# Mixing layers of a two-block network: the order of VectorE's rotation, the recurrence's products and two weight splits

## The chip, the cores and the metric

The kernel runs on one core of one Trainium2 chip. The metric is the device time of one execution in microseconds (us), lower is better. The core has a matrix engine (TensorE, PE in the profile), a vector engine (VectorE, DVE), a scalar engine (ScalarE, ACT), GpSimd (POOL), and SyncE (SP), which issues the DMAs.

## The reference, cut to what matters

A first block (attention, pooling, a mixture of 32 experts) is followed by a second block of two layers. Only the mixing part of each of these two layers is touched by the change:

```python
def second_block(x, positions, attn_norm_w, w_in, ..., w_out, ...):
    for layer in range(2):
        h = rms_norm_2(x, attn_norm_w[layer])                    # x: (1, 256, 1024)
        a_q, a_i, a_zf, a_zb, a_g, b_u, c_q, c_k, c_v = jnp.split(h @ w_in[layer], SPLIT_POINTS, axis=-1)
        o_a = hgrn2_mixer(a_q, a_i, a_zf, a_zb, a_g, lb_all[layer])   # a gated recurrence, both directions
        o_b = fourier_mixer(b_u)
        o_c = dilated_attention_mixer(c_q, c_k, c_v, positions)       # q, k rotated; 8 heads of 64
        x = x + jnp.concatenate([o_a, o_b, o_c], axis=-1) @ w_out[layer]
        ...                                                           # squared-ReLU feed-forward
    return rms_norm_2(x, final_norm_w)
```

## The kernel before, in words

All products are made in fp32r, with each operand as a high part and a low part. `split` makes them for a 128x1024 piece of the weights: ACT writes the high part `wh`, DVE the low part `wl` (L203, two instructions of 128x512 where a norm weight is folded in; L207, one of 128x1024, for `w_out`). Four pairs of `wh`/`wl` buffers take turns.

`mix_layer` runs six projections one after the other: `proj(512)` z, `proj(0)` q and i of the recurrence, `proj(1536)` Q, `proj(2048)` K, `proj(2560)` V, `proj(1024)` gate and Fourier input, and then the output projection by `w_out`. A projection has four blocks on PE, each of 12 matmuls of 128x512 (L230 to L232: `wh` twice, `wl` once, for two row tiles and two slices), with one `split` each. Here the blocks behind the K projection are called **A, B, C, D** (V) and **E, F, G, H** (gate); the names of their low parts are `wl_5307`, `5403`, `5450`, `5534`, `5586`, `5655`, `5693`, `5744`.

After each block, `bg()` advances every generator in the list `bgs` by one step and so puts other work between the blocks:

- `hgrn`, the recurrence as eight levels `lv` 0 to 7. A level is `qt` (DVE, L1509) and `kt` (POOL, L1513), then small matmuls (`hsm`, L1483, up to level 4; `diag`, L1526, levels 5 and 6; `cross`, level 7), for `hsm` a masked copy `sl` (DVE, L1490) and its sum `sd` (POOL, L1491), and the updates `hES` (L1545) and `hIP` (L1546) on DVE for the next level.
- `turn`, of Q and of K. The evacuation `evac_rot` multiplies the projection by cosine and sine on DVE (`rx` L1605, `rt` L1606, two row tiles) and adds the two (L1607: the first tile on POOL, the second on DVE). `turn` transposes the result on PE (`prot`, L1617) and copies it on ACT.
- `attention`, in four softmax pieces called here **a, b, c, d** (tiles `s_5386`, `5432`, `5517`, `5563`; sums `l_5392`, `5438`, `5523`, `5569`): scores on PE (`sc` L1643), scale and mask on DVE (L1648), maximum on DVE (L1651), its negative on POOL (L1652), exp on ACT (L1656), reciprocal on DVE (L1657), and four multiplications on POOL (L1660). Then, for each of two groups, `values`: transposes of the weights on PE (`pt` L1671), copies `pT` on DVE and ACT (L1672), and the product with V (`po` L1680).

Every engine takes its instructions in a fixed order, which a scheduler settles when the kernel is built, from the order of the code, priorities and dependences; an instruction that waits holds up all behind it on its engine. The layer 1 part repeats that of layer 0, 310.3 us later.

Of the kernel before, what the change touches and what calls it, by code (L numbers as in the profile page):

```python
# [115 lines left out]
class Kernel:  # L116
    def __init__(self, tc, a):
# [2 lines left out]
        self.last_load = None  # L120
        self.smalls = []


    def add_ring(self, st, n, cols=4096, **kw):

# [89 lines left out]
    def halves(self, v, g=None):  # L215

        for hh in range(2):
            hi, lo = self.split(v[:, 2 * hh:2 * hh + 2, :].rearrange("p k f -> p (k f)"),
                                g if g is None else g[:, 2 * hh:2 * hh + 2])
            for k2 in range(2):  # L220
                yield 2 * hh + k2, hi, lo, k2 * 512

# [1176 lines left out]
    def mix_layer(self, layer, rc, late):  # L1399
# [3 lines left out]
        with ExitStack() as st:  # L1403
# [6 lines left out]
            hT, mT = self.hT, self.mT  # L1410
            win = a["w_in_2"][layer]
            gw = self.norm_cols("attn_norm_w_2", 1) if layer else self.g0
            tk = {}

            def tok(name, n=512, tag="tk", bufs=2):
                tk[name] = p.tile([128, 2, n], F32, name=name, tag=tag, bufs=bufs)
# [32 lines left out]
            def hgrn():  # L1449
# [50 lines left out]
                for lv in range(8):  # L1500
# [5 lines left out]
                        return x.rearrange("p n (b w h) -> p (n b) w h", w=2, h=h)[:, :, w]  # L1506

                    for d in range(2):
                        nc.vector.tensor_tensor(half(qt, 1 - d), half(qd, 1 - d), half(IP[:, d], 1 - d), op=ALU.mult)  # L1509
                        if lv == 0:  # L1510
                            nc.scalar.copy(half(kt, d), half(kk[:, d], d))
                        else:
                            nc.gpsimd.tensor_tensor(half(kt, d), half(kk[:, d], d), half(ES[:, d], d), op=ALU.mult)  # L1513
# [25 lines left out]
                    if lv < 7:  # L1539

                        for d in range(2):
                            edge = (lambda x: x[:, :, h - 1:h]) if d == 0 else (lambda x: x[:, :, 0:1])
                            full = [128, 2 * S // (2 * h), h]
                            ip, es = IP[:, d], ES[:, d]
                            nc.vector.tensor_tensor(half(es, d), half(es, d), edge(half(ip, 1 - d)).to_broadcast(full), op=ALU.mult)  # L1545
                            nc.vector.tensor_tensor(half(ip, 1 - d), half(ip, 1 - d), edge(half(ip, d)).to_broadcast(full), op=ALU.mult)  # L1546
                    yield
                while not tail:
# [49 lines left out]
            def evac_rot(dst, gens, steps):  # L1598

                def g(c0, ps):  # L1600
                    rx = p.tile([128, 2, 8, 2, 32], F32, name="rx", tag="rx", bufs=1)
                    for t in range(2):
                        x = ps[t].rearrange("p (h w c) -> p h w c", h=8, w=2)
                        tmp = p.tile([128, 8, 2, 32], F32, name="rt", tag="rt", bufs=2)
                        nc.vector.tensor_tensor(rx[:, t], x, cos[:, t].unsqueeze(1).unsqueeze(1).to_broadcast([128, 8, 2, 32]), op=ALU.mult)  # L1605
                        nc.vector.tensor_tensor(tmp, swapped(x), sin[:, t].unsqueeze(1).to_broadcast([128, 8, 2, 32]), op=ALU.mult)  # L1606
                        (nc.vector if t else nc.gpsimd).tensor_tensor(rx[:, t], rx[:, t], tmp, op=ALU.add)  # L1607

                    def turn():
                        for _ in range(steps):  # L1610
                            yield
                        for m in range(0, 4, 2):
                            ps = bank((128, 2, S), "prot")
                            for i in range(2):
                                for t in range(2):
                                    src = rx[:, t, 2 * (m + i):2 * (m + i) + 2].rearrange("p h w c -> p (h w c)")
                                    nc.tensor.transpose(ps[:, i, t * 128:(t + 1) * 128], src, self.ident)  # L1617
                            nc.scalar.copy(dst[:, m:m + 2], ps)
                        yield
                    gens.insert(0, turn())  # L1620
                return g

            def evac_cv(c0, ps):
# [37 lines left out]
                    yield  # L1661

            def values(g):
                pTs = []
                for kt in range(2):
                    pT = p.tile([128, 2, 2, S], F32, name="pT", tag="pT", bufs=2)
                    for j in range(2):
                        pt = bank((128, 2, S), "pt")
                        for t in range(2):
                            for i in range(2):  # L1670
                                nc.tensor.transpose(pt[:, i, t * 128:(t + 1) * 128], probs[g][t][:, j, i, kt * 128:(kt + 1) * 128], self.ident)  # L1671
                        (nc.scalar.copy if j else nc.vector.tensor_copy)(pT[:, j], pt)  # L1672
                    pTs.append(pT)
                    yield
                po = bank((128, 2, S), "po2")
                for i in range(2):
                    for kt in range(2):
# [32 lines left out]
                    into_mT(2 + m, ps)  # L1710
                yield

            bgs, tail = [], []

            def bg():
                for w in list(bgs):
                    if next(w, 0) == 0:
                        bgs.remove(w)

            def proj(c0, e, late=()):  # L1720
                ps = [bank() for _ in range(2)]
                self.tok_part(ps, hT, win, 0, c0, True, False, bg, g=gw[:, 0:4])
                for f in late:
                    f()
                self.tok_part(ps, hT, win, 4, c0, False, True, bg, g=gw[:, 4:8])
                e(c0, ps)

            proj(512, evac_z, late)
            if not layer:
# [5 lines left out]
            hg = hgrn()  # L1735
            bgs.append(hg)
            proj(0, evac_qi)
            proj(1536, evac_rot(qT, bgs, 1))
            proj(2048, evac_rot(kT, bgs, 0))
            att = attention()  # L1740
            bgs.append(att)
            proj(2560, evac_cv)
# [5 lines left out]
            bg()  # L1748
            wo = a["w_out_2"][layer]
            acc = [[bank(name="wo") for _ in range(2)] for _ in range(2)]  # L1750
            for n in range(2):
                self.tok_part(acc[n], mT, wo, 4, n * 512, True, False, bg)
            while bgs:
# [148 lines left out]
```

## Time and profile before

| | us |
|---|---|
| median of 3 runs (1305.76 to 1309.66) | 1307.24 |
| the profiled execution | 1306.97 |
| its span (first to last instruction) | 1305.2 |
| PE busy in the span | 1253.0 |
| DVE busy | 680.5 |
| ACT busy | 510.7 |
| POOL busy | 200.7 |

The mean granted TensorE clock of the span is 0.989 of full speed. PE is busy 96% of the span, so what can be won or lost is idle time of PE, time at a lower clock, and the order in which other engines release it. A timeline row has the start of a group of like instructions, the time from its first start to its last end, engine, line, and in brackets the idle time before it with what ended it. Neighbouring instructions overlap a little, so that the distance between two starts is less than the first one's duration.

### The profile page before, as it was taken

The page shows a single profiled execution, that of the slowest core. Times are in us where ns is not written, and L with a number is a line of the kernel's source. Part 1 is how long each engine was busy: PE and PEld are TensorE (multiplying, and loading weights), DVE is VectorE, ACT ScalarE, POOL GpSimd, SP SyncE. Part 2 cuts the span into 40 slices and gives each one's busy share as a digit, 9 for nine tenths or more (in the row PEclk, how much of TensorE's full clock was granted, in tenths as well). Part 3 has the DMA queues.
Part 4 walks back from the last instruction along what each step waited for, and adds up shares of the span by engine and source line. Part 5 has one row for each costly group of instructions (what it writes and reads, how often), then busy time and mean ns, then how long its engine had stood idle before and what let it go on. Part 6 is the DMA issues. An engine that isn't in the chain of part 4 may idle for free. (4 is left out here: it accounts for less than half of the span.)

```text
span 1305.2 us, 19758 instructions
## 1 busy us (share of the span) xinstructions
PE 1253.0 (96%) x7985; PEld 875.2 (67%) x7985; DVE 680.5 (52%) x1164; ACT 510.7 (39%) x919; POOL 200.7 (15%) x270
## 2 busy tenths in 40 slices
PE   6999988999999999899999999999999999999997
PEld 3889976344443443333357678998988767989896
DVE  3698797122122221212157965655557994765654
ACT  2456433111110111101056465555556555655544
POOL 0011030000000000000024541211113461211211
PEclk9999998999999999999999999999999999999999
DMA  9998797999999999999975342655554423555550
GB/s 326 372 340 276 266 381 266 409 416 429 426 429 427 426 427 427 426 428 421 419 305 187 114 130 90 223 181 186 193 193 158 161 82 126 188 177 193 193 162 33
DMA packets 102597, 359.37 MB, mean 275 GB/s; under 512 B 8772, under 2 KB 17856, under 8 KB 87656
## 3 DMA queue, kind: packets, MB, share of 16 engines
q1 hardware_dynamic: 101832, 357.00, 72.1%
q8 instruction: 63, 1.03, 0.3%
q0 software_dynamic: 480, 1.07, 0.2%
q14 instruction: 30, 0.25, 0.1%
q10 hardware_dynamic: 192, 0.02, 0.0%
HBM read 357.00 MB, written 1.06 MB: 274 GB/s over the span
## 5 line engine op out<-in xcount | busy, mean ns | idle before, releaser
L207 DVE TENSOR_TENSOR wl<-w,wh 128x1024 fp32r<-128x1024 f32 x128 | 156.5, 1227 | 100.9 <-ACT wh L206 100.9
L206 ACT CAST wh<-w 128x1024 fp32r<-128x1024 f32 x128 | 134.1, 1050 | 144.4 <-PE up L241 65.8
L202 ACT ACTIVATE wh<-w,vcols 128x512 fp32r<-128x512 f32 x176 | 121.2, 718 | 78.9 <-PE dn L231 34.7
L203 DVE SCALAR_TENSOR_TENSOR wl<-w,vcols,wh 128x512 fp32r<-128x512 f32 x176 | 131.1, 778 | 36.5 <-ACT wh L202 34.4
L241 PE MATMUL up<-hT,wh 128*128 128x256 f32 x512 | 142.4, 278 | 0.0
L242 PE MATMUL up<-hT,wl 128*128 128x256 f32 x512 | 142.4, 279 | 0.0
L240 PE MATMUL up<-hT,wh 128*128 128x256 f32 x512 | 142.4, 278 | 0.0
L1015 PE MATMUL pu<-w,xT 128*64 128x512 f32 x512 | 121.5, 608 | 5.4 <-DMA w<-in_w_expert_up_dram 5.4
L1015 PE MATMUL pg<-w,xT 128*64 128x512 f32 x512 | 119.5, 604 | 0.0
L1101 ACT CAST yh<-y 128x512 fp32r<-128x512 f32 x32 | 19.8, 618 | 253.6 <-DVE y L1100 187.9
L1015 PE MATMUL py<-w,actT 128*64 128x512 f32 x480 | 108.0, 593 | 1.4 <-DMA w<-in_w_expert_down_dram 1.4
L231 PE MATMUL dn<-wh,actl 128*128 128x512 f32 x256 | 101.3, 396 | 0.0
L230 PE MATMUL dn<-wh,acth 128*128 128x512 f32 x256 | 101.2, 395 | 0.0
L232 PE MATMUL dn<-wl,acth 128*128 128x512 f32 x256 | 101.2, 396 | 0.0
L241 PEld LDWEIGHTS up<-hT,wh 128*128 128x128 f32 x512 | 96.9, 189 | 0.6
L240 PEld LDWEIGHTS up<-hT,wh 128*128 128x128 f32 x512 | 96.2, 188 | 0.6
L242 PEld LDWEIGHTS up<-hT,wl 128*128 128x128 f32 x512 | 96.0, 188 | 0.5 <-DVE wl L203 0.5
L1803 POOL TENSOR_TENSOR relu<-relu 128x256 f32<-128x256 f32 x64 | 53.6, 838 | 265.9 <-ACT relu L1802 265.9
L230 PE MATMUL b<-wh,hT 128*128 128x512 f32 x224 | 92.0, 412 | 2.4 <-ACT wh L202 1.9
L232 PE MATMUL b<-wl,hT 128*128 128x512 f32 x224 | 89.4, 403 | 2.3 <-DVE wl L207 1.5
L1100 DVE SCALAR_TENSOR_TENSOR y<-py,ws,gate 128x512 f32<-128x512 f32 x30 | 22.5, 751 | 128.7 <-PE py L1015 127.2
L1015 PEld LDWEIGHTS pu<-w,xT 128*64 128x64 f32 x512 | 38.0, 139 | 76.9 <-issue 67.1
(411 smaller groups left out, 2273.3 us busy)
## 6 DMA issues: line engine op xcount, KB each, us to landing
w<-in_w_expert_up_dram SPq DMA_DIRECT2D x26, 2048.0 KB, 25.7
w<-in_w_expert_down_dram SPq DMA_DIRECT2D x26, 2048.0 KB, 27.2
w<-in_w_expert_gate_dram SPq DMA_DIRECT2D x24, 2048.0 KB, 25.4
w<-in_w_in_dram SPq DMA_DIRECT2D x40, 1024.0 KB, 6.5
w<-in_w_up_dram SPq DMA_DIRECT2D x32, 1024.0 KB, 5.4
w<-in_w_down_dram SPq DMA_DIRECT2D x32, 1024.0 KB, 5.0
w<-in_w_ada_dram SPq DMA_DIRECT2D x24, 1024.0 KB, 9.8
w<-in_w_expert_gate_dram SPq DMA_DIRECT2D x16, 1024.0 KB, 10.3
```

The source lines that it names most:

```text
L202: self.nc.scalar.activation(hi[:, c], v[:, c], AF.Copy, scale=g[:, i:i + 1])
L203: self.nc.vector.scalar_tensor_tensor(lo[:, c], v[:, c], g[:, i:i + 1], hi[:, c].bitcast(F32), op0=ALU.mult, op1=ALU.subtract)
L206: self.last_hi = self.nc.scalar.copy(hi, v).ins
L207: self.last_lo = self.nc.vector.tensor_tensor(lo, v, hi, op=ALU.subtract).ins
L230: nc.tensor.matmul(ps, hT.tok(0, k, t), wh, start=first, stop=False)
L231: nc.tensor.matmul(ps, hT.tok(1, k, t), wh, start=False, stop=False)
L232: nc.tensor.matmul(ps, hT.tok(0, k, t), wl, start=False, stop=last)
L240: nc.tensor.matmul(o, hi[:, c], hT.mov(0, k), start=first and m % 2 == 0, stop=False, skip_group_check=True)
L241: nc.tensor.matmul(o, hi[:, c], hT.mov(1, k), start=False, stop=False, skip_group_check=True)
L242: nc.tensor.matmul(o, lo[:, c], hT.mov(0, k), start=False, stop=last and m % 2 == 1, skip_group_check=True)
L1015: queue["last"] = f(*args, **kw).ins
L1803: nc.gpsimd.tensor_tensor(r, r, r, op=ALU.mult)
```

## The change

It has three parts, alike in both layers. (1) In the projections of Q and K, `turn` stands behind the recurrence in `bgs` and takes one step more before it transposes, and the last `bg()` of the projection runs behind the evacuation (`first=True`). (2) `behind(...)` holds an instruction behind given ones in the issue order of its engine: the recurrence's `qt` and `hES` behind the latest rotation's last add (`turned[-1:]`, on DVE), and the second split of the next projection behind the same add (`split_after[1]`). (3) The first split of the output projection is held behind the `pT` copies of the first group's second half (`split_after[0]`).

```diff
+    def behind(self, *ins):
+        st = ExitStack()
+        for i in ins:
+            st.enter_context(self.tc.issue_after(i))
+        return st
...
         for hh in range(2):
-            hi, lo = self.split(v[:, 2 * hh:2 * hh + 2, :].rearrange("p k f -> p (k f)"),
-                                g if g is None else g[:, 2 * hh:2 * hh + 2])
+            with self.behind(*self.split_after.pop(hh, ())):
+                hi, lo = self.split(v[:, 2 * hh:2 * hh + 2, :].rearrange("p k f -> p (k f)"),
+                                    g if g is None else g[:, 2 * hh:2 * hh + 2])
...
-            tk = {}
+            tk, turned = {}, []
...
-                        nc.vector.tensor_tensor(half(qt, 1 - d), half(qd, 1 - d), half(IP[:, d], 1 - d), op=ALU.mult)
+                        with self.behind(*turned[-1:]):
+                            nc.vector.tensor_tensor(half(qt, 1 - d), half(qd, 1 - d), half(IP[:, d], 1 - d), op=ALU.mult)
...
-                            nc.vector.tensor_tensor(half(es, d), half(es, d), edge(half(ip, 1 - d)).to_broadcast(full), op=ALU.mult)
+                            with self.behind(*turned[-1:]):
+                                nc.vector.tensor_tensor(half(es, d), half(es, d), edge(half(ip, 1 - d)).to_broadcast(full), op=ALU.mult)
...
-                        (nc.vector if t else nc.gpsimd).tensor_tensor(rx[:, t], rx[:, t], tmp, op=ALU.add)
+                        last = (nc.vector if t else nc.gpsimd).tensor_tensor(rx[:, t], rx[:, t], tmp, op=ALU.add).ins
+                    turned.append(last)
+                    self.split_after[1] = (last,)
...
-                    gens.insert(0, turn())
+                    gens.insert(1, turn())
...
-                        (nc.scalar.copy if j else nc.vector.tensor_copy)(pT[:, j], pt)
+                        copies.append((nc.scalar.copy if j else nc.vector.tensor_copy)(pT[:, j], pt).ins)
                     pTs.append(pT)
                     yield
+                if not g:
+                    copied.extend(copies[2:])
...
-            def proj(c0, e, late=()):
+            def proj(c0, e, late=(), first=False):
...
-                self.tok_part(ps, hT, win, 4, c0, False, True, bg, g=gw[:, 4:8])
+                steps = [bg]
+                if not first:
+                    steps.append(bg)
+                self.tok_part(ps, hT, win, 4, c0, False, True, lambda: steps and steps.pop()(), g=gw[:, 4:8])
                 e(c0, ps)
+                if first:
+                    bg()
...
-            proj(1536, evac_rot(qT, bgs, 1))
-            proj(2048, evac_rot(kT, bgs, 0))
+            proj(1536, evac_rot(qT, bgs, 2), first=True)
+            proj(2048, evac_rot(kT, bgs, 1), first=True)
...
+            self.split_after[0] = copied
```

The order on PE differs only around the two rotations. At that of K, behind block A of layer 0 (`b_5303` and `b_5304` are the two row tiles of the V projection, `rx` the rotated K), before:

```order
L1617 MATMUL prot_5324<-ident_69,rx_5294 128x128
L1617 MATMUL prot_5330<-ident_69,rx_5294 128x128
L1483 MATMUL hsm_5336<-qt_5288,kt_5289 32x32 x8
L1617 MATMUL prot_5324<-ident_69,rx_5294 128x128 x3
L1617 MATMUL prot_5330<-ident_69,rx_5294 128x128 x3
L1483 MATMUL hsm_5336<-qt_5288,kt_5289 32x32 x8
L1483 MATMUL hsm_5356<-qt_5288,kt_5289 32x32 x16
L1643 MATMUL sc_5380<-kT_4680,qT_4679 128x256
L1643 MATMUL sc_5381<-kT_4680,qT_4679 128x256
L1643 MATMUL sc_5380<-kT_4680,qT_4679 128x256
L1643 MATMUL sc_5381<-kT_4680,qT_4679 128x256
L230 MATMUL b_5303<-wh_5402,hT00_78 128x512
```

and of the change, from the second of the four `wh` matmuls of block B (its first `wl` matmul is the last row):

```order
L240 MATMUL b_5303<-wh_5402,hT10_80 128x512
L239 MATMUL b_5304<-wh_5402,hT00_78 128x512
L240 MATMUL b_5304<-wh_5402,hT10_80 128x512
L1492 MATMUL hsm_5324<-qt_5297,kt_5298 32x32 x16
L1492 MATMUL hsm_5344<-qt_5297,kt_5298 32x32 x16
L1630 MATMUL prot_5368<-ident_69,rx_5288 128x128 x4
L1630 MATMUL prot_5374<-ident_69,rx_5288 128x128 x4
L1656 MATMUL sc_5380<-kT_4680,qT_4679 128x256
L1656 MATMUL sc_5381<-kT_4680,qT_4679 128x256
L1656 MATMUL sc_5380<-kT_4680,qT_4679 128x256
L1656 MATMUL sc_5381<-kT_4680,qT_4679 128x256
L241 MATMUL b_5303<-wl_5403,hT00_78 128x512
```

The first four matmuls of block B have moved ahead of the recurrence and the transposes, and the recurrence ahead of the transposes. At the rotation of Q it is the same without `sc`, where before the transposes stood behind a whole block and the recurrence another block later.

On DVE the rotation now stands ahead of `qt` and `hES`, and this moves what follows. Around the third reciprocal (`l_5523`, piece c), before:

```order
L1657 RECIPROCAL l_5523<-l_5523 128x4
L1545 TENSOR_TENSOR hES_4677<-hES_4677,hIP_4676 128x4x64
L1651 TENSOR_REDUCE mx_5566<-s_5563 128x4
L1546 TENSOR_TENSOR hIP_4676<-hIP_4676 128x4x64
L1545 TENSOR_TENSOR hES_4677<-hES_4677,hIP_4676 128x4x64
L203 SCALAR_TENSOR_TENSOR wl_5744<-w_4683,g0_748,wh_5743 128x512
L1546 TENSOR_TENSOR hIP_4676<-hIP_4676 128x4x64
L203 SCALAR_TENSOR_TENSOR wl_5744<-w_4683,g0_748,wh_5743 128x512
L1672 COPY pT_5641<-pt_5642 128x512
L1509 TENSOR_TENSOR qt_5761<-hq_4678,hIP_4676 128x2x128
```

and of the change:

```order
L1670 RECIPROCAL l_5523<-l_5523 128x4
L1556 TENSOR_TENSOR hES_4677<-hES_4677,hIP_4676 128x8x32
L1664 TENSOR_REDUCE mx_5566<-s_5563 128x4
L1557 TENSOR_TENSOR hIP_4676<-hIP_4676 128x8x32
L1556 TENSOR_TENSOR hES_4677<-hES_4677,hIP_4676 128x8x32
L211 SCALAR_TENSOR_TENSOR wl_5655<-w_4683,g0_748,wh_5654 128x512
L1557 TENSOR_TENSOR hIP_4676<-hIP_4676 128x8x32
L1685 COPY pT_5641<-pt_5642 128x512
L1670 RECIPROCAL l_5569<-l_5569 128x4
L211 SCALAR_TENSOR_TENSOR wl_5655<-w_4683,g0_748,wh_5654 128x512
```

Where the split of block H (`wl_5744`) stood between the third reciprocal and the fourth, the split of block F (`wl_5655`) stands now, its first half between them and its second half behind the fourth (`l_5569`); before, F's split stood ahead of the second reciprocal. The recurrence's updates there are those of one level earlier.

On POOL, from the multiplications of piece a on, before:

```order
L1660 TENSOR_SCALAR s_5386<-s_5386,l_5392 128x256 x4
L1491 TENSOR_TENSOR sd_4965<-sd_4965,sl_5484 128x128
L1491 TENSOR_TENSOR sd_4965<-sd_4965,sl_5504 128x128
L1513 TENSOR_TENSOR kt_5673<-hk_4675,hES_4677 128x4x64 x2
L1660 TENSOR_SCALAR s_5432<-s_5432,l_5438 128x256 x4
L1652 TENSOR_SCALAR mx_5520<-mx_5520 128x4
L1660 TENSOR_SCALAR s_5517<-s_5517,l_5523 128x256 x4
L1652 TENSOR_SCALAR mx_5566<-mx_5566 128x4
L1513 TENSOR_TENSOR kt_5762<-hk_4675,hES_4677 128x2x128 x2
L1660 TENSOR_SCALAR s_5563<-s_5563,l_5569 128x256 x4
```

and of the change:

```order
L1673 TENSOR_SCALAR s_5386<-s_5386,l_5392 128x256 x4
L1500 TENSOR_TENSOR sd_4965<-sd_4965,sl_5484 128x128
L1500 TENSOR_TENSOR sd_4965<-sd_4965,sl_5504 128x128
L1673 TENSOR_SCALAR s_5432<-s_5432,l_5438 128x256 x4
L1523 TENSOR_TENSOR kt_5552<-hk_4675,hES_4677 128x8x32 x2
L1665 TENSOR_SCALAR mx_5520<-mx_5520 128x4
L1673 TENSOR_SCALAR s_5517<-s_5517,l_5523 128x256 x4
L1665 TENSOR_SCALAR mx_5566<-mx_5566 128x4
L1673 TENSOR_SCALAR s_5563<-s_5563,l_5569 128x256 x4
L1523 TENSOR_TENSOR kt_5673<-hk_4675,hES_4677 128x4x64 x2
L1523 TENSOR_TENSOR kt_5762<-hk_4675,hES_4677 128x2x128 x2
```

The `kt` of level 5 (8x32) has moved from ahead of piece a to behind piece b, and that of level 6 (4x64) from ahead of piece b to behind piece d. SP's order of loads is as before. The three splits of `w_out` behind the first group's copies now stand together on DVE.

## Rows read from the trace of the kernel before

**Rows 1.** Windows: length, busy PE PEld DVE ACT POOL (count), PEclk, DMA share, GB/s.
```profile
705.00:732.70 27.70, 27.70 (x368) 21.91 (x366) 27.20 (x54) 13.19 (x23) 12.80 (x15) 1.00 0.42 131
...
738.00:740.40 2.40, 2.40 (x56) 1.74 (x56) 2.00 (x5) 0.58 (x1) 1.74 (x4) 0.55 0.02 7
...
765.00:770.00 5.00, 4.00 (x32) 2.50 (x29) 4.56 (x7) 3.13 (x6) 4.78 (x4) 1.00 0.77 236
```

**Rows 2.** Timeline of PE: start, duration, instruction, [idle before <-releaser].
```profile
722.59 1.03 PE L1617 MATMUL prot<-ident,rx 128*128 128x128 f32 x8
...
735.66 0.44 PE L1617 MATMUL prot<-ident,rx 128*128 128x128 f32 x2 [2.90 <-POOL rx L1607]
...
738.62 1.87 PE L1643 MATMUL sc<-kT,qT 64*128 64x256 f32 x8
740.41 0.50 PE L230 MATMUL b<-wh,hT 128*128 128x512 f32 x1
...
743.37 1.13 PE L1643 MATMUL sc<-kT,qT 64*128 64x256 f32 x8
...
747.41 0.76 PE L1483 MATMUL hsm<-qt,kt 64*32 64x32 f32 x64
...
1045.99 0.44 PE L1617 MATMUL prot<-ident,rx 128*128 128x128 f32 x2 [2.90 <-POOL rx L1607]
```

**Rows 3.** Timeline of DVE, same columns.
```profile
732.99 0.68 DVE L1605 TENSOR_TENSOR rx<-b,cosr 128x512 f32<-128x512 f32 x1
...
735.82 0.68 DVE L1607 TENSOR_TENSOR rx<-rx,rt 128x512 f32<-128x512 f32 x1
...
749.28 0.76 DVE L203 SCALAR_TENSOR_TENSOR wl<-w,g,wh 128x512 fp32r<-128x512 f32 x1
...
759.03 0.18 DVE L1657 RECIPROCAL l<-l 128x4 f32<-128x4 f32 x1 [2.44 <-ACT s L1656]
...
761.30 0.88 DVE L203 SCALAR_TENSOR_TENSOR wl<-w,g,wh 128x512 fp32r<-128x512 f32 x1
...
762.44 1.23 DVE L203 SCALAR_TENSOR_TENSOR wl<-w,g,wh 128x512 fp32r<-128x512 f32 x1
...
764.52 0.17 DVE L1657 RECIPROCAL l<-l 128x4 f32<-128x4 f32 x1
```

**Rows 4.** Timeline of POOL, same columns.
```profile
722.59 2.04 POOL L1513 TENSOR_TENSOR kt<-hk,hES 128x256 f32<-128x256 f32 x2
...
734.34 1.26 POOL L1607 TENSOR_TENSOR rx<-rx,rt 128x512 f32<-128x512 f32 x1 [0.69 <-DVE rt L1606]
...
748.01 3.54 POOL L1660 TENSOR_SCALAR s<-s,l 128x256 f32<-128x256 f32 x4
...
752.54 1.42 POOL L1513 TENSOR_TENSOR kt<-hk,hES 128x256 f32<-128x256 f32 x2
753.94 2.71 POOL L1660 TENSOR_SCALAR s<-s,l 128x256 f32<-128x256 f32 x4
...
759.30 2.35 POOL L1660 TENSOR_SCALAR s<-s,l 128x256 f32<-128x256 f32 x4 [2.49 <-DVE l L1657]
...
764.79 4.99 POOL L1660 TENSOR_SCALAR s<-s,l 128x256 f32<-128x256 f32 x4 [0.52 <-DVE l L1657]
```

**Rows 5.** Timeline of PE around the fifth to seventh block.
```profile
753.18 0.51 PE L230 MATMUL b<-wh,hT 128*128 128x512 f32 x1
...
756.15 0.76 PE L1526 MATMUL diag<-qt,kt 64*32 64x32 f32 x64
...
757.69 0.47 PE L230 MATMUL b<-wh,hT 128*128 128x512 f32 x1
...
760.52 1.03 PE L1671 MATMUL pt<-ident,s 128*128 128x128 f32 x8
...
766.79 1.51 PE L1680 MATMUL po<-pT,cv 128*64 128x256 f32 x12 [1.00 <-DVE pT L1672]
```

**Rows 6.** DMA issues, 690 to 800 us: KB each, median us to landing.
```profile
w<-in_w_out_dram SPq DMA_DIRECT2D x4, 1024.0 KB, 5.1
```

More of the change, by code (lines that the diff above doesn't have):

```diff
@@ L121, in __init__ @@
         self.smalls = []
+        self.split_after = {}
+    def behind(self, *ins):
[3 more added lines that the diff above has]
+        return st
     def add_ring(self, st, n, cols=4096, **kw):
@@ L1663, in values @@
             def values(g):
-                pTs = []
+                pTs, copies = [], []
                 for kt in range(2):
@@ L1711, in fourier @@
                 yield
-            bgs, tail = [], []
+            bgs, tail, copied = [], [], []
             def bg():
```

## The prediction

> **What bounds the kernel now.** The engine shares came first: PE is busy for 1253.0 of the span's 1305.2 us (the table above), so a gain can only come from the gaps and the clock. Then the windows of one mixing layer. From 705 to 732.7 us PE has no gap and its granted clock is 1.00 [rows 1]. Then, at the rotation of K, PE idles 2.90 us for the rotation's add [rows 2], and the clock falls to 0.55 from 738 to 740.4 us [rows 1], between the chip's two levels of 1.2 and 2.4 GHz. The same gap stands 310.3 us later in the second layer [rows 2], so everything below counts twice. At the rotation of Q there is none: the transposes at 722.59 us begin at once [rows 2]. The only other gap that the change touches is 1.00 us at the first product with V [rows 5]; no fall of the clock goes with it (1.00 from 765 to 770 us, [rows 1]). Last I followed the softmax through DVE and POOL, because the order rows show it moved: reciprocal c waits 2.44 us for the exp [rows 3], and POOL multiplies in four stretches of 2.35 to 4.99 us [rows 4]. It is a chain with little slack, not counted by PE's share.
>
> Times below are on the axis of layer 0 in the trace of before.
>
> **The change at the two rotations.** Block A starts at 735.66 − 2.90 − 2.83 = 729.93 us (2.83 is one block, 757.69 to 760.52, [rows 5]), and block B ends at 743.37 [rows 2]: 13.4 us. With the change, kt decides when PE goes on: the rotation's first two DVE steps (0.60 each by the starts, row length 0.68, [rows 3]), then POOL's add, 1.26, and two kt, 2.04 [rows 4], make 4.5 us from the start of A, if the rotation starts there. PE arrives after A and the four moved matmuls, 2.83 + 0.92 = 3.75: a wait of 0.75 (0.4 to 1.0, as kt is between 1.42 and 2.04, [rows 4], and the rotation starts a little behind A). Then 0.76 for hsm, 1.03 for eight transposes, 0.4 for the copy of K (none shown here; between 0 and the 0.68 of a 128x512 pass), 1.13 for the scores and 1.83 for the other eight matmuls [rows 2]. The sum is 9.65 us, so K gains 3.8. Q has the same wait, which it did not have, and its splits follow later on DVE: it costs 0.8 (0.5 to 1.5). At the end of B PE is **3.0 us ahead**, and the scores of piece a end at 738.5 instead of 740.41: 1.9 us earlier (1.0 to 4.0, the latter if every wait above vanished). If nothing else moved, the change would gain 3.0 us a layer.
>
> **What lies behind it.** From the end of the first scores to POOL's first multiplication of piece a it takes 748.01 − 740.41 = 7.6 us on DVE, POOL and ACT, and this doesn't get shorter: it starts at about 746.1. Then 4.5 us to the end of a and its two sd (748.01 to 752.54), 2.7 for b and 1.42 for two kt, in before kt first, after it b first, so 754.7 either way for the negated maximum of c [rows 4]. Reciprocal c came 2.4 us after that (756.65 to 759.03), so now at about 757.1. PE meets this line first: block E, 2.97 us, would start at 753.18 − 3.0 and end at 753.2, and the diag behind it now waits for the kt behind b until 754.7. It took 1.54 from diag to F, so F starts at 756.3 [rows 5], only 1.4 us ahead of before. Here half of the lead is gone.
>
> **The new wait.** Block F needs the first half of its low part at its third matmul, 0.46 later, at 756.8. In before that split was made ahead of reciprocal b and waited for nobody. Now it stands behind reciprocal c, two updates of the recurrence and maximum d. In before the split in this place (H's) ended 762.11 − 759.03 = 3.1 us behind reciprocal c [rows 3]; it hid there, since H comes two blocks later. So the half is ready at 757.1 + 3.1 = 760.2, and **PE waits 3.4 us**. The second half stands behind reciprocal d. That came 5.5 us behind c (764.52 − 759.03), and nothing of this changes: maximum d, its negative behind POOL's c, the exps. So d is at 762.6 and the half at 763.4 with one split of 0.76 [rows 3]. PE comes to its use at about 761.9, waits 1.5 more, and ends F with four matmuls at 764.4. In before F ended at 760.52 [rows 5]. F is **3.9 us late**. Its range is 1.8 (scores that end 4.0 instead of 1.9 earlier) to 4.8 (1.0 earlier).
>
> Behind F the low parts of G and H come in one row on DVE, ahead of PE. The diag of level 6 follows a block, a transposition and G later, near 768.1; its kt stands behind POOL's d. That starts 0.27 after reciprocal d and lasts 2.35 to 4.99 us, with 1.42 of kt 766.6 to 769.3 [rows 4]: hidden up to 1.2 us, which I leave to the range. The 1.00 us gap at the product with V goes, because PE is later than the copies: **−1.0**.
>
> The clock: after 2.90 us without work the stretch from 735.66 to 740.41 took 4.75 us, where its rows at full clock (1.03, 0.76, 1.13) make 2.92 [rows 2]. A gap of 1.00 us cost nothing [rows 1]. The new wait of 3.4 us is nearer the former: **+1.6**, with 0 and 3.2 (paid at both waits in F) as bounds; the 1.8 of the old gap also held a short wait. The gain at K above has the end of the old price in it.
>
> The third part of the change, the output projection's splits, puts three passes of 128x1024 together ahead of DVE's copies of the mixed output. PE is busy with other blocks meanwhile: **+0.3** as an estimate, between nothing, where they are hidden, and 1.4, somewhat over the 1.23 of the longest split here (762.44, [rows 3]). The ring of weights is freed later, but a load lands 5.1 us after its issue [rows 6] and SP issues in the same order; its data are used tens of us later. Nothing is charged; if that cover were gone, the price would be F's lag, 3.9 us a layer.
>
> Sum of a layer against before: 3.9 − 1.0 + 1.6 + 0.3 = **4.8 us slower**, two layers 9.6. The profiled execution took 1306.97 us, 0.27 below the median of the runs shown and 1.77 above its span, so 1306.97 + 9.6 = **1316.6 us**.
>
> **A rule that would make it dearer.** The split that PE waits for in F's second half now runs while POOL multiplies d. In the trace a split beside POOL's multiplication took 0.76 us (749.28, with POOL busy from 748.01, [rows 3, 4]), as it does alone, and one beside kt took 1.23 (762.44, [rows 3]). The Trainium skill, "SBUF — State Buffer", section "Who interferes with whom", says that a DVE instruction that reads two SBUF inputs and a GpSimd instruction lock each other out for the whole of whichever came first. The first of the two rows doesn't agree with it for POOL's multiplications, the second does for kt. By the rule the half would wait for one of POOL's four multiplications of d, up to 4.99/4 = 1.2 us, on average 0.6 a layer: 1317.8 us.
>
> **The rivals.**
> - *Faster: the softmax chain runs much quicker once DVE waits.* POOL's multiplications take 0.59 us each in c and 0.88 in a for the same work [rows 4]; if DVE's work beside them is what lengthens them and the kt, and DVE now stands idle before its reciprocals, the chain shrinks. Where it decides: each us by which reciprocals c and d come before 757.1 and 762.6 takes one from F's 3.9, and the 1.6 of the clock falls away; a gain of 2 a layer needs 5.2 us, F wholly on time 6.9. For it: all of a, b and c at c's pace save 1.6 us, and scores that end 4.0 earlier instead of 1.9 save 2.1. Against: that is 3.7, not 5.2, and reciprocal c waits 2.44 us for exps in the trace of before too [rows 3]. With F on time: 3.9 − 6.9 − 1.0 + 0.3 = 3.7 faster a layer, 1299.6 us.
> - *No change: the lead is just eaten.* If POOL's a runs like c (1.2 us less) and its b too (0.4), and the scores come 0.7 earlier than I put them, the reciprocals come 2.3 us earlier; F's first wait is then 1.1, too short for the clock: 4.8 − 2.3 − 1.6 = 0.9 a layer, 1308.8 us.
> - *Dearer: kt of level 6 is late too.* If POOL's d takes its 4.99 us again, the diag waits 1.2 us for kt behind it, and the clock is paid twice (1.6 more) and the tail 1.1 more: 8.5 to 8.7 a layer, 1324 us.
> - *The price is paid by POOL, not DVE.* Were the kt behind b 2.07 instead of 1.42, both diags move by 0.65; it is inside the first forecast's range.
>
> **Numbers.** The forecast, F waits for DVE in both halves, 60%: 1311 to 1320.5 us. Dearer 13%: 1320.5 to 1326. No change in kind, 17%: 1303 to 1311. Faster, 10%: 1296 to 1303. A measurement here can tell 0.3%, 3.9 us, from no change, so 1303.3 to 1311.2 counts as the same. Slower has 73%, the same 17%, faster 10%. The range of eight in ten leaves out the faster case, the lower half of the no-change case and the upper part of the dearer one: 1307.5 to 1322.
>
> **What would show it.** In the trace after: no 2.90 us gap before the transposes of K but a wait under 1.0 before hsm, on POOL's kt, at both rotations; the clock at 1.00 there; the scores of a some 2 us earlier; diag of 32x32 waiting for kt; then two gaps in block F released by DVE's wl of L211, the larger 2 to 4 us, with the clock falling behind it; no gap before the product with V. I am wrong if block F runs without a gap (then reciprocal d is much earlier than 762.6), if PE's gap at the rotations is as long as before, or if the clock doesn't fall behind F's wait (then 3.2 us less).

## The result and the profile after

The changed kernel takes 1321.57 us (median of 4 runs, 1320.04 to 1325.64) against 1307.24: the ratio is 1.011, with a 95% interval of 1.0092 to 1.0128. It is slower, on the forecast's side and inside its range (1307.5 to 1322), but by 14.3 us where 9.6 was forecast.

All of it lies in the two mixing layers, and more than the difference of the two profiles shows. In the trace a layer's **mixing stretch**, from the start of the recurrence's first small products (`hsm<-hq`) to that of the feed-forward's first product (`up`), is 99.48 us before (708.99 to 808.47; second layer 99.46) and 107.62 after (705.88 to 813.50; second layer 107.61): **8.14 us a layer**, 16.3 in both. The feed-forward layers agree to 0.02 us. The first block happened to end some 3 us sooner in the profile after, and such differences of the first block come and go between profiles (the stretch of layer 0 starts at 705.2 to 714.1 us in those of the runs below); the stretch repeats to 0.03 us between the two layers unless the clock falls. So the runs below are read by it, beside their times.

PE's gaps of layer 0 after, those of more than 0.5 us, with the rows that answer to [rows 2] and [rows 5] (the axis is 3.11 us ahead of that of before):

```profile
717.95 0.75 PE L1492 MATMUL hsm<-qt,kt 64*32 64x32 f32 x64 [1.03 <-DVE qt L1519]
...
720.26 0.73 PE L241 MATMUL b<-wl,hT 128*128 128x512 f32 x2 [0.54 <-DVE wl L211]
...
723.53 0.51 PE L241 MATMUL b<-wl,hT 128*128 128x512 f32 x1 [0.70 <-DVE wl L211]
...
734.28 0.75 PE L1492 MATMUL hsm<-qt,kt 64*32 64x32 f32 x64 [0.85 <-DVE qt L1519]
...
747.76 0.50 PE L241 MATMUL b<-wl,hT 128*128 128x512 f32 x1 [1.29 <-DVE wl L211]
...
752.62 0.50 PE L241 MATMUL b<-wl,hT 128*128 128x512 f32 x1 [0.57 <-DVE wl L211]
...
755.12 0.76 PE L1536 MATMUL diag<-qt,kt 64*32 64x32 f32 x64
...
759.88 0.50 PE L241 MATMUL b<-wl,hT 128*128 128x512 f32 x1 [2.51 <-DVE wl L211]
...
762.90 0.80 PE L241 MATMUL b<-wl,hT 128*128 128x512 f32 x1 [0.95 <-DVE wl L211]
...
764.78 1.91 PE L1684 MATMUL pt<-ident,s 128*128 128x128 f32 x8
```

At K the gap of 2.90 us is gone, with 0.85 in its place, and at Q there are now three (1.03, 0.54, 0.70). F waits twice for its split, 2.51 and 0.95. The windows of the same trace tell what the clock did:

```profile
709.50:717.95 8.45, 7.42 (x93) 5.86 (x93) 5.89 (x10) 3.93 (x6) 4.42 (x5) 1.00 0.00 0
734.00:737.30 3.30, 2.78 (x80) 2.21 (x80) 3.30 (x9) 1.07 (x2) 1.79 (x4) 1.00 0.00 0
759.88:764.78 4.90, 3.95 (x11) 2.56 (x12) 3.63 (x8) 2.55 (x9) 2.48 (x4) 0.61 0.16 13
764.78:766.34 1.56, 1.56 (x10) 1.56 (x8) 1.17 (x2) 0.00 (x0) 1.56 (x3) 0.50 1.04 400
```

It stays at 1.00 through the rotations and falls to half behind F's wait: the transposes at 764.78 take 1.91 us instead of 1.03. On DVE, with the rows that answer to [rows 3]:

```profile
710.08 0.58 DVE L1499 TENSOR_TENSOR sl<-hsm,kmix 128x128 f32<-128x128 f32 x2 [3.08 <-PE hsm L1492]
712.61 0.69 DVE L1616 TENSOR_TENSOR rx<-b,cosr 128x512 f32<-128x512 f32 x1 [1.95 <-PE b L241]
...
715.74 2.06 DVE L1519 TENSOR_TENSOR qt<-hq,hIP 128x256 f32<-128x256 f32 x2
...
732.32 1.82 DVE L1519 TENSOR_TENSOR qt<-hq,hIP 128x256 f32<-128x256 f32 x2
...
746.95 1.64 DVE L211 SCALAR_TENSOR_TENSOR wl<-w,g,wh 128x512 fp32r<-128x512 f32 x2
...
756.68 0.18 DVE L1670 RECIPROCAL l<-l 128x4 f32<-128x4 f32 x1 [1.78 <-ACT s L1669]
...
758.95 0.88 DVE L211 SCALAR_TENSOR_TENSOR wl<-w,g,wh 128x512 fp32r<-128x512 f32 x1
...
762.03 0.18 DVE L1670 RECIPROCAL l<-l 128x4 f32<-128x4 f32 x1 [1.27 <-ACT s L1669]
762.12 0.72 DVE L211 SCALAR_TENSOR_TENSOR wl<-w,g,wh 128x512 fp32r<-128x512 f32 x1
...
771.52 3.48 DVE L215 TENSOR_TENSOR wl<-w,wh 128x1024 fp32r<-128x1024 f32 x3
774.92 0.41 DVE L313 TENSOR_TENSOR mT<-po,mT 128x256 fp32r<-128x256 f32 x1
```

DVE now stands idle *ahead* of Q's rotation, 3.08 and 1.95 us: the recurrence's `qt` and `hES`, which it did there before, may not run until the rotation is through. And when they run, a pair of `qt` takes 2.06 and 1.82 us instead of about 0.75. POOL, answering to [rows 4], shows what runs beside it:

```profile
715.23 2.29 POOL L1523 TENSOR_TENSOR kt<-hk,hES 128x256 f32<-128x256 f32 x2
...
731.80 2.04 POOL L1523 TENSOR_TENSOR kt<-hk,hES 128x256 f32<-128x256 f32 x2
...
745.99 2.95 POOL L1673 TENSOR_SCALAR s<-s,l 128x256 f32<-128x256 f32 x4
...
752.00 2.30 POOL L1523 TENSOR_TENSOR kt<-hk,hES 128x256 f32<-128x256 f32 x2
...
762.30 3.52 POOL L1673 TENSOR_SCALAR s<-s,l 128x256 f32<-128x256 f32 x4 [2.42 <-DVE l L1670]
765.80 1.41 POOL L1523 TENSOR_TENSOR kt<-hk,hES 128x256 f32<-128x256 f32 x2
```

The `kt` of 715.23 and 731.80 cover all but the last 0.3 us of those `qt`. From the start of the stretch to the first mixed output (`mT`, 774.92) DVE's gaps in this trace add up to 9.0 us, against 3.2 in the trace of before, and its pass for that output starts 69.04 us into the stretch instead of 59.99, behind three passes of the output projection's split (771.52).

### The profile page after: what moved, and what is told of

Its sections match the earlier page's. It is cut to its first block, busy times and chain, and to the rows that moved or that the text cites. A ratio compares the mean times of both kernels' runs of the same rounds, so it can differ in the third digit from the quotient of the medians.

```text
span 1318.4 us, 19762 instructions
## 1 busy us (share of the span) xinstructions
PE 1255.7 (95%) x7985; PEld 873.7 (66%) x7985; DVE 686.2 (52%) x1164; ACT 510.8 (39%) x919; POOL 199.2 (15%) x270
## 3 DMA queue, kind: packets, MB, share of 16 engines
q8 instruction: 63, 1.03, 0.3%
HBM read 357.00 MB, written 1.06 MB: 272 GB/s over the span
## 5 line engine op out<-in xcount | busy, mean ns | idle before, releaser
L211 DVE SCALAR_TENSOR_TENSOR wl<-w,vcols,wh 128x512 fp32r<-128x512 f32 x176 | 129.1, 767 | 36.7 <-ACT wh L210 34.6
L239 PE MATMUL b<-wh,hT 128*128 128x512 f32 x224 | 92.4, 414 | 2.2 <-ACT wh L210 1.7
L240 PE MATMUL b<-wh,hT 128*128 128x512 f32 x224 | 89.9, 401 | 0.0
```

The lines of the kernel that those rows point to most:

```text
L211: self.nc.vector.scalar_tensor_tensor(lo[:, c], v[:, c], g[:, i:i + 1], hi[:, c].bitcast(F32), op0=ALU.mult, op1=ALU.subtract)
L239: nc.tensor.matmul(ps, hT.tok(0, k, t), wh, start=first, stop=False)
L240: nc.tensor.matmul(ps, hT.tok(1, k, t), wh, start=False, stop=False)
```

## The experiments

The table gives the start of some PE work in layer 0, in us from the start of the stretch, each read as the difference of two starts in a run's trace. A, C, F, G and H are blocks, f is the first Fourier product, up the end of the stretch, in both layers. A stretch is that of one execution, the ratio that of all. For x2 to x7 the two agree to 0.7 us of a kernel; for the change, x1 and x8 to x12 the times are 1.3 to 2.6 us lower against before than the stretches say, and what makes that difference was not looked for.

| run | A | C | F | G | H | f | up, layer 0 / 1 | ratio to before (95%) |
|---|---|---|---|---|---|---|---|---|
| before | 20.86 | 35.44 | 48.70 | 52.32 | 59.25 | 68.56 | 99.48 / 99.46 | |
| the change | 23.72 | 34.60 | 50.78 | 60.46 | 66.83 | 76.70 | 107.62 / 107.61 | 1.011 (1.0092 to 1.0128) |
| x1 order only | 20.86 | 36.50 | 49.74 | 53.37 | 60.41 | 69.71 | 100.64 / 100.26 | 0.9999 (0.9982 to 1.0017) |
| x2 no recurrence hold | 22.10 | 35.78 | 49.02 | 52.64 | 62.20 | 73.02 | 103.96 / 102.40 | 1.0052 (1.0033 to 1.0071) |
| x3 rotation on DVE | 23.21 | 33.54 | 49.96 | 58.03 | 63.75 | 75.90 | 106.86 / 106.72 | 1.011 (1.0091 to 1.0129) |
| x4 K only | 20.88 | 31.74 | 47.95 | 56.18 | 61.88 | 73.89 | 104.83 / 104.81 | 1.0079 (1.006 to 1.0098) |
| x5 F's split first | 23.67 | 34.54 | 50.75 | 54.38 | 62.14 | 74.65 | 105.60 / 106.15 | 1.0093 (1.0073 to 1.0113) |
| x6 K only, F's split first | 20.91 | 31.78 | 47.95 | 51.58 | 59.33 | 71.83 | 102.82 / 102.83 | 1.0053 (1.0032 to 1.0074) |
| x7 holds only | 21.82 | 32.41 | 47.67 | 56.10 | 61.82 | 74.20 | 105.12 / 104.72 | 1.0083 (1.0064 to 1.0102) |
| x8 third part only | 20.87 | 36.64 | 49.92 | 53.55 | 59.62 | 69.37 | 100.31 / 100.01 | 0.9998 (0.9982 to 1.0014) |
| x9 x6, mixed output first | 20.86 | 31.72 | 47.91 | 51.53 | 59.32 | 68.71 | 99.61 / 99.63 | 0.9985 (0.9971 to 0.9999) |
| x10 x9, kt ahead of d | 20.91 | 31.76 | 47.95 | 51.57 | 57.66 | 66.97 | 97.91 / 97.91 | 0.9959 (0.9945 to 0.9974) |
| x11 x10, both rotations | 23.70 | 34.57 | 50.76 | 54.38 | 60.49 | 69.79 | 100.71 / 101.24 | 1.0003 (0.9988 to 1.0018) |
| x12 x10, K's add on DVE | 20.86 | 31.18 | 47.58 | 51.20 | 57.20 | 66.51 | 97.45 / 97.48 | 0.9959 (0.9943 to 0.9976) |

**x1, the order of the generators alone.** The change without `behind(...)` on `qt` and `hES` and without both `split_after`.

> Only the order of the generators is kept (the rotation's transposes behind the recurrence, the last step behind the evacuation); the recurrence's qt and hES, the second split and the output projection's split are held behind nothing. Theory A (the loss comes from what DVE does behind the holds: F's split behind reciprocals c and d, qt beside kt): four matmuls and hsm slide into the old 2.90 us gap at K, F's split is made ahead of reciprocal b as before, no gap in block F; 1.5 to 3.5 us a layer faster than before, 1300 to 1304 us. Rival B (the new order on PE itself costs, above all at Q's rotation): slower than before by 2 us a layer or more, 1311 us or above.

A miss: F waits for nothing, as theory A has it, but nothing is gained. The rotation ends when it did (first transposes 26.7 us into the stretch in both traces), so the work slid into the gap leaves a gap of 2.24 and one of 0.56 us, and the clock falls for longer behind them, to 0.50 for 6 us where before it was 0.54 for 3.2. That makes the stretch 1.2 and 0.8 us longer, and the times show no difference:

```profile
730.50:733.60 3.10, 0.33 (x1) 0.14 (x1) 3.10 (x7) 0.43 (x1) 1.49 (x2) 0.92 0.25 95
733.60:739.60 6.00, 6.00 (x20) 4.36 (x21) 6.00 (x12) 1.17 (x2) 3.17 (x5) 0.50 0.21 62
740.00:742.00 2.00, 2.00 (x12) 1.42 (x12) 2.00 (x4) 0.67 (x2) 0.72 (x1) 1.00 0.69 268
```

**x2, no hold of the recurrence.**

```diff
-                        with self.behind(*turned[-1:]):
-                            nc.vector.tensor_tensor(half(qt, 1 - d), ...)
+                        nc.vector.tensor_tensor(half(qt, 1 - d), ...)
```

and the same at `hES`.

> The change without the hold of qt and hES behind the rotation; the two holds of splits stay. Theory A: F's split stands ahead of reciprocal c and qt does not run beside kt at the rotations, so most of the 8.1 us a layer is gone: within 2 us a layer of before, 1303 to 1311 us; the gap in F is under 1 us. Rival B (PE's order costs): 1316 us or above. A hold of splits that costs by itself would show as gaps of PE for wl in blocks A to D and 1311 to 1316 us.

Between theory A and rival B. K's gap is back (2.15 us for POOL's add), F has none, and PE now waits 2.33 us (2.65 in the second layer) at the product with V for a `pT` copy on DVE. Blocks A to D have no gap for `wl`; one of 0.93 us stands ahead of A, which starts 1.24 us late. Of the loss of 8.14 us a layer 4.48 and 2.94 are left, so the hold of `qt` and `hES` makes about half of it, and DVE is late at the end without it too.

**x3, the rotation wholly on DVE.**

```diff
-                        last = (nc.vector if t else nc.gpsimd).tensor_tensor(rx[:, t], ...)
+                        last = nc.vector.tensor_tensor(rx[:, t], ...)
```

> The change, with the first tile's add of the rotation on DVE too instead of POOL; every other instruction keeps its place. kt then starts before the rotation ends and is done when qt begins. Theory C (qt takes 0.9 to 1.0 us instead of 0.37 because it runs at the same time as POOL's kt): the two qt behind each rotation take 0.75 us together instead of 2.06 and 1.82, PE's waits for qt (1.03 and 0.85 us) shrink to 0.3 or less, and the kernel gains 1 to 3 us a layer on the change: 1315.5 to 1319.5 us. Rival (qt is slow for what it reads or for its place): qt stays at 1.8 us or more a pair, the rotation is 0.6 us longer on DVE, 1321 to 1324 us.

`qt` answered at once; PE's wait for it fell from 1.03 and 0.85 us to 0.32 at both places:

```profile
717.83 0.75 DVE L1519 TENSOR_TENSOR qt<-hq,hIP 128x256 f32<-128x256 f32 x2
...
721.97 1.82 DVE L1519 TENSOR_TENSOR qt<-hq,hIP 128x256 f32<-128x256 f32 x2
...
733.83 0.75 DVE L1519 TENSOR_TENSOR qt<-hq,hIP 128x256 f32<-128x256 f32 x2
...
737.96 1.83 DVE L1519 TENSOR_TENSOR qt<-hq,hIP 128x256 f32<-128x256 f32 x2
```

The two pairs that POOL's `kt` no longer covers take 0.75 us, the two that it still covers 1.82. That decides for theory C as to `qt`. The whole gains 0.8 us a layer, and the time of 1321.50 us is no better than the change's, so the gain that was expected is missed: the rest of the loss is not made here.

**x4, the change at K alone.** Q keeps `steps` 1, its place in `bgs` and its last `bg()` ahead of the evacuation, and sets neither `turned` nor `split_after`.

> The change at K's rotation only; Q's rotation has the order of before (transposes first, nothing held behind it). F's split stays behind reciprocals c and d. Theory A with its ledger: Q's loss of 2.9 us a layer goes, the softmax chain starts that much earlier, the gap in F stays within 1 us of 3.5: 1315 to 1317.5 us. If the gap in F were set by the distance between PE and the chain, an earlier PE would only wait longer in F: 1319 us or above. If Q were the whole loss: 1305 us.

Q's 2.8 us a layer go: 8.14 becomes 5.35, and the time of 1318.43 us is 0.9 above what was expected. Behind Q the parts change places and their sum stays: F to G takes 1.45 us less than in the change, G to H 0.67 less, H to f 2.14 more, since PE now waits at the end for `mT` (0.76) and for a copy (0.86).

**x5, F's split first.** `tok_part` makes both splits of E and F before E's matmuls, and the reciprocals of c and d are issued behind them (`norms` has the reciprocal and POOL's multiplications of c and of d, `self.folded` is here the last low part of F's split); the order on PE is untouched.

```diff
+        if c0 == self.ahead and not kb:
+            parts = list(parts)
...
+                for f in norms:
+                    with self.behind(self.folded):
+                        f()
```

> The change, with reciprocals c and d issued on DVE behind the split of block F, whose two halves then stand together ahead of them; the order on PE is the same, instruction for instruction. The measure is a layer's mixing stretch, from the recurrence's first small products to the first product of the feed-forward: 99.48 us before, 107.62 with the change. Theory A (F's wait for its split, and the clock behind it, is most of the loss): no gap above 0.5 us in block F, the clock stays at 1.00, E still ends 2.1 us late and F 2 to 3 us late, the stretch takes 101 to 104 us and the kernel 1311 to 1315 us. Rival D (the end of the stretch is set by the chain on DVE behind reciprocal d: splits of G and H, the recurrence, three splits of the output projection): F's gap goes, but gaps come at the products with V and at cross, the stretch stays at 106 to 108 us and the kernel at 1319 to 1322 us.

My theory fell here. F's gap and the fall of the clock are gone (F takes 3.63 us from its start to G's instead of 9.68), yet 6 of the 8 us stay. F starts 2.05 us late, as in the change, G adds 0.83, and 3.20 come between H and f, as rival D has it, with 1.27 us before the second half of `cross` for the mixed output and 0.86 for a copy behind it. On DVE that output, `mT`, stands behind the three passes of the output projection's split:

```profile
773.62 1.13 PE L1550 MATMUL cross<-qt,kt 64*128 64x128 f32 x8 [1.27 <-DVE mT L317]
...
777.86 1.51 PE L1704 MATMUL po<-pT,cv 128*64 128x256 f32 x10 [0.86 <-ACT pT L1694]
```

```profile
768.80 3.48 DVE L216 TENSOR_TENSOR wl<-w,wh 128x1024 fp32r<-128x1024 f32 x3
772.21 0.41 DVE L317 TENSOR_TENSOR mT<-po,mT 128x256 fp32r<-128x256 f32 x1
```

**x6, K alone with F's split first** (x4 and x5 together).

> The change at K's rotation alone, with F's split ahead of reciprocals c and d as in the run beside it. Theory A: E ends 0.7 us earlier than before, F without a gap, the stretch takes 98 to 100.5 us, 1304 to 1309 us. Rival D: the stretch stays within 1 us of the 104.8 us that the change at K alone took, 1317 to 1319 us.

Up to H PE is now level with before (59.33 against 59.25), and 3.2 of the 3.3 us lost stand between H and f. The stretch of 102.82 us lies between the two forecasts: F's gap is worth more here than rival D allowed, and less than theory A did.

**x7, the holds alone**, in the order of generators of before.

> All holds of the change (qt, hES, the second split, the output projection's split) with the order of the generators of before. Theory A (DVE idles ahead of each rotation, since the recurrence's work may not run there, and does it later): the rotation of K comes some 3 us earlier, but PE waits for it behind block A as before, 1.5 to 2.5 us; the waits in blocks D to F stay, the stretch takes 107 to 110 us, 1322 to 1328 us. Rival (holds cost only together with the new order): 100 to 103 us, 1308 to 1314 us.

Smaller than I expected: K's gap is 0.54 us, not 1.5 to 2.5. The rotation starts on DVE 1.5 us sooner than before (22.52 us into the stretch against 24.00) and A 1.0 later. But the loss of 5.6 and 5.3 us that remains comes with PE's old order: F waits 2.94 us for its split. With x1, which has the new order and loses 1.2 and 0.8, it shows that the holds, and not the order of PE, make most of the loss.

**x8, the third part alone.**

> The kernel before with the third part of the change alone (the first split of the output projection behind the copies of the first group's second half). All theories here: the two gaps that it could open are at the products with V and at cross; 99.3 to 100.0 us a stretch, 1306 to 1309 us. If the third part made the gaps at the end of the stretch, it would show them here too, with 100.5 us or more.

By its time the third part does nothing. From A to C this trace loses 1.2 us, where the same gap at K (2.91 us) has a longer stretch at the low clock behind it; from G to H it gains the 0.9 of the old gap at the product with V, and from H to f it loses 0.4. The end is not opened by it as long as DVE is on time.

**x9, the mixed output ahead of the output projection's splits**, on x6.

```diff
                 for i in range(2):
                     into_mT(4 + 2 * g + i, po[:, i])
+                if not g:
+                    copied.append(self.mixed)
```

> As the change at K alone with F's split first (102.82 us a mixing stretch), with the three splits of the output projection held behind the low part of the mixed output of the first group instead of ahead of it on DVE; the order on PE is the same. Theory D (the end of the stretch is set by DVE reaching the mixed output late, with three passes of 1.2 us ahead of it): the gap of 1.27 us at cross and the one of 0.86 us behind it go, the stretch takes 99.5 to 100.5 us and the kernel 1306 to 1310 us. Rival (DVE's backlog is as long whatever comes first, and the splits are then late for the output projection): gaps move to the output projection's first matmuls, 102 to 103.5 us and 1312 to 1316 us.

The gaps at `cross` and behind it go, 3.2 us a layer, with the same order on PE: theory D was right.

**x10, also POOL's `kt` of level 6 ahead of its multiplications of d.**

```diff
+                    if kt and not g:
+                        with self.behind(self.kt):
+                            norms[1]()
```

> As the run beside it, with POOL's kt of level 6 ahead of its multiplications of piece d. Theory D: PE's wait of 0.64 us for this kt ahead of the diag goes, 98.8 to 99.8 us a stretch, level with before or up to 1 us a layer ahead of it: 1304 to 1308 us. Rival (the pieces that PE transposes last are then late): a gap of 0.5 to 1.5 us at the third pt, 100 us or more.

Better than expected: PE's wait for `kt` goes and G's for its split too. The gaps that are left in the stretch are these four, and the kernel beats the one before by 0.4%:

```profile
736.94 0.75 PE L1496 MATMUL hsm<-qt,kt 64*32 64x32 f32 x64 [0.85 <-DVE qt L1523]
...
738.95 1.14 PE L1661 MATMUL sc<-kT,qT 64*128 64x256 f32 x8 [0.24 <-ACT kT L1636]
...
750.42 0.50 PE L242 MATMUL b<-wl,hT 128*128 128x512 f32 x1 [1.28 <-DVE wl L212]
...
755.27 0.50 PE L242 MATMUL b<-wl,hT 128*128 128x512 f32 x1 [0.56 <-DVE wl L212]
```

**x11, the same repairs with the change at both rotations; x12, with K's first add on DVE.**

> The whole change, at Q's rotation too, with the three repairs (F's split ahead of reciprocals c and d, the mixed output ahead of the output projection's splits, kt of level 6 ahead of piece d). The ledger: only Q's loss of 2.86 us a layer is left against the run with K alone (97.91 us a mixing stretch): 100.3 to 101.2 us, 1309 to 1312 us. Rival (Q's loss is slack that the later blocks take up): 98 to 99 us, 1304 to 1307 us.

> The change at K alone with the three repairs, and the first tile's add of K's rotation on DVE, so that POOL's kt is done before qt begins. Theory C (qt beside kt is what makes PE wait 0.85 us): the pair of qt takes 0.75 instead of 1.82 us, the wait falls to 0.3, the stretch gains 0.3 to 0.6 on 97.91 us. Rival: the longer rotation on DVE (0.6 us) eats it, 97.8 to 98.2 us.

In x11 A starts 2.8 us late, and 2.8 (3.3 in the second layer) is all that parts it from x10: Q's loss is no slack that later blocks take up. The 0.5 us more of the second layer are a fall of the clock at Q, shown in the last section. In x12 the pair of `qt` takes 0.75 us, hsm waits 0.31, and the stretch gains 0.45, within what was expected; the times can't tell it from x10.

## Why the prediction was right, and where it was mis-sized

The differences of the first two rows of the table add up to the loss of layer 0: to A +2.86 (Q), A to C −3.70 (K), C to F +2.92, F to G +6.06, G to H −0.56, H to f +0.56: 8.14.

- **K's rotation: right in size, not in what makes it.** Gain 3.8 forecast, 3.70 measured; the clock stays at 1.00, and the wait is 0.85 us, for `qt` and not for `kt`. The sum let the rotation start with block A, and that is what the holds bring: with the holds and the old order on PE A to C gains 3.99 (x7), with the new order and no hold it loses 1.06 (x1).
- **Q's rotation: the step that failed.** "it costs 0.8 (0.5 to 1.5)" measured 2.86, outside its bounds. I costed the chain rotation, add, `kt`, `hsm` as if DVE had nothing else to do, and named POOL's `kt` as what PE waits for. It waits for `qt`, which the hold puts behind the add and beside `kt` (x3), and then twice for `wl` that DVE makes late. [Rows 1] had the warning: DVE was busy for 27.20 of 27.70 us there. To forbid it work in such a stretch is to leave it idle (3.08 and 1.95 us) and to do the work later. The order alone costs Q nothing (x1: A starts at 20.86, as before), the holds alone 0.96 (x7), the order with the holds of splits 1.24 (x2); the 2.86 take all of them together.
- **Hence the softmax chain starts no earlier.** The first pass over the scores on DVE starts 33.21 us into the stretch against 31.52, behind another pair of `qt` of 1.84 us, and not 1.9 us earlier; reciprocal c comes 50.80 us into the stretch against 50.04, where the forecast had 48.1.
- **C to F: a loss of lead as forecast, but 2.92 for 1.6, and for another reason.** I had diag wait for POOL's `kt` of level 5. That is ready (752.00 and 2.30, against 755.12); blocks D and E wait for their own splits, 1.29 and 0.57 us, which I had not listed.
- **F's wait: right in place and kind.** Two gaps released by L211, of 2.51 and 0.95 us (forecast 3.4 and 1.5); the half is done 3.07 us behind reciprocal c (3.1), and d follows c by 5.35 (5.5). PE reaches F 3.5 us later than forecast and reciprocal c comes 2.7 later: that both slipped alike, behind one late DVE, is what kept this wait near the forecast.
- **The clock: +1.6 was low.** F to G costs 6.06 in layer 0, of which 3.46 are the gaps; the other 2.6 are matmuls at a clock of 0.61 and 0.50, and some 0.4 follow in G. In the second layer F to G costs 4.64 with one gap of 2.52, so 2.1.
- **The tail: +0.3 hides a second bound.** H to f costs 0.56 in layer 0. In the second layer H starts only 5.52 us late, and yet it ends 8.15 late, since PE then waits for `mT` and a copy, as in x5. I took the three splits of the output projection for hidden work. They are, while DVE is on time (x8), and cost 3.2 us when it is not (x6 against x9). So the terms don't add up as I added them: what PE loses at F by the clock it doesn't lose at the end. Layer 0 of x3, without a fall of the clock, takes 106.86 us, and layer 1, with it, 106.72.
- **The sum.** 4.8 a layer was right in sign and short by 3.3: Q 2.1 more, C to F 1.3 more, the clock 1.4, the tail 0.3, less 1.4 for a shorter wait in F and 0.3 that F's own steps did not hold.
- **The luck in it.** The 1321.57 us lie in the range, 0.4 from its end, but above the 1311 to 1320.5 that I gave to F's wait and inside those of the dearer rival, whose sign, a diag of level 6 that waits for `kt`, isn't there (769.93, no gap). And F's wait makes only some 2 of the 8 us: with F on time I put the change 3.7 us a layer faster, yet x5 without that wait is 6.1 slower than before, and x6, where F also starts 0.75 ahead of before, 3.3. With F, the mixed output and `kt` all mended, Q's loss keeps the stretch 1.2 and 1.8 us behind (x11), though the time can't be told from before. The sign came out right in part by terms that I had put too small.

The Trainium skill's rule on the shared port ("SBUF — State Buffer", "Who interferes with whom") I weighed at F's second half, as a wait of DVE behind POOL's multiplications. It is the other way round: the half started first (762.12, POOL's d from 762.30) and took 0.72 us, as alone, and it is POOL that took longer. Its eight multiplications of c and d, all alike, took from 0.47 to 1.14 us, and the longest is the one that began beside this half (a row of the view by line: shortest, median and longest in ns, then the first and last start):

```profile
L1673 POOL TENSOR_SCALAR s<-s,l x8: 473/762/1142, 757.0 to 764.9; 128x256 f32<-128x256 f32 x8
```

So the trace agrees with the rule, also where DVE and POOL both multiply two tensors and POOL is first: `qt` beside `kt`, 1.82 and 2.06 us against 0.75 (x3 and x12), a place that I had not looked at. And the prediction read its first row there, the split of 0.76 us (749.28), from DVE's side alone: POOL's multiplications beside it took 3.54 us against 2.35 in c [rows 4]. No run separates that price of POOL's from the rest.

Open: which part of x2's loss is the second split's hold and which the end's backlog was not taken apart, and the second split's hold was never run by itself; nor was a form sought in which Q's rotation gains too.

## What to carry to other kernels

Before an instruction is held behind another, read how busy its engine is in that stretch: here DVE was 98% busy, and the hold bought the first wait with idle time that came due at later waits on DVE. Price the hold and the new order apart, each in a run of its own: here the holds made both the gain at K and the loss. Look for the bound behind the bound: F's gap was plain in the trace and its removal gave back only 2 of 8 us, because DVE's backlog met PE again at the mixed output. And read a stage by a stretch of the trace with fixed ends: it told 0.45 us a layer apart (x12 from x10), where the intervals of the times are some 2 us of a kernel to either side.

## What the runs showed of the hardware that was not expected

The clock doesn't follow the gaps alone. In x3 block F has gaps of 2.54 and 1.35 us in layer 0 and no fall, while in layer 1, with the same order and gaps of 2.51 and 1.29, the mean is 0.60:

```profile
761.00:766.00 5.00, 3.65 (x21) 2.78 (x20) 3.73 (x7) 2.46 (x10) 3.02 (x4) 1.00 0.22 50
1078.50:1084.00 5.50, 4.21 (x15) 3.05 (x14) 4.03 (x7) 2.28 (x9) 3.38 (x4) 0.60 0.28 77
```

In x11 gaps of 1.03, 0.54 and 0.68 us at Q left the clock at 1.00 in layer 0, and those of 1.03 and 0.54 brought it to 0.50 in layer 1, some 16 us into the stretch in both, which cost 0.59 us at A:

```profile
726.00:728.00 2.00, 1.32 (x6) 0.76 (x6) 2.00 (x3) 1.34 (x2) 0.58 (x1) 1.00 0.71 205
1038.00:1040.00 2.00, 2.00 (x6) 1.59 (x5) 2.00 (x4) 0.11 (x1) 0.94 (x2) 0.50 0.50 131
```

And the same gap at K (2.90, 2.91 us) had the low clock behind it until 740.4 us in before, 31.4 into the stretch; in x8 the mean from 31.7 to 35 us into the stretch is still 0.73, and A to C takes 1.2 us longer. So the 1.8 us of the prediction would have been 3.0 there: a price for such a gap, read from one place, is good to a factor of two.
